# Short constant products of TensorE in the waits at the beginning and end of two mixture-of-experts layers

## Chip, cores, metric

One core of a Trainium2 chip runs the whole program in one launch. The metric is the device time of a run in microseconds (us); lower is better. Five engines work side by side and wait for each other through semaphores: TensorE (PE; its weight loads are PEld), VectorE (DVE), ScalarE (ACT), GpSimd (POOL) and SyncE (SP, which issues most DMAs).

## What is computed

The reference is a chain of ten layers on 256 tokens of width 1024, in float32: gated linear attention, a mixture of experts (MoE), differential attention, a second MoE, and then twice a feed-forward layer, a mixer and a feed-forward layer. A layer norm stands behind each. The change sits in the two MoE layers:

```python
g_idx = jnp.argmax(g_logits, axis=-1)              # one of 4 groups for each token
top_w, top_i = lax.top_k(jax.nn.softmax(e_logits, axis=-1), 2)   # 2 of the group's 4 experts
...
for e in range(16):
    hdn = jax.nn.silu(t @ w_gate[e]) * (t @ w_up[e])
    y = y + combine[:, e:e + 1] * (hdn @ w_down[e])
```

## The kernel before

**Number format.** Large products run in a fast form of float32: each operand is split into a high part (ACT, a cast) and a low part (DVE, a subtraction; POOL for a few) by `split`, line 107. A product is then three matmuls (hi x hi, lo x hi, hi x lo). A matmul of plain float32 operands, such as the router's, is carried out as two PE instructions. A transpose is one PE instruction against the identity matrix `ident`.

**Weights.** They come in units of 128 x 2048 values (1 MB), one DMA each (line 85, on SP's queue), through a ring of five raw buffers and four split ones. In an MoE `GU` (line 696) multiplies the tokens of a group with an expert's gate and up weights, 512 columns a matmul, and `down` (`mm3`, lines 102 to 104) with the down weights.

**Where an MoE begins** (`moe`, `LN`). The layer norm before it (`_rows`, lines 227 to 241) works on one block of 128 tokens after the other (tb is 0, then 1): DVE adds, ACT squares, POOL takes the root, DVE scales. Eight transposes of a block follow (line 250), ACT copies them out (line 734), and `logits` (line 534) makes 20 router values for each token: 8 float32 products with 20 columns, so 16 PE instructions. `route` picks the group on DVE (lines 539 to 548, with small products at line 546 that count the tokens before each one), and `slots` (line 551) makes the matrix `Pm` that picks a group's tokens. `gather` (line 614) multiplies by it, ACT and DVE copy the rows out (line 615), `gathered_T` (line 622) transposes them, `split` parts them, and `GU` of expert 0 begins. POOL splits the two blocks of activations meanwhile (`xl`, line 107), and DVE the second weight unit.

**Where an MoE ends.** After expert 15's `down` (line 104 is its last matmul) ACT and DVE split the sum (`y_parts`). A branch, `tc.If` at line 791, skips the case of groups over 128 tokens; each engine reads the count and takes the branch itself. `scatter` (lines 644 and 645) then multiplies back into token order, and the next layer's first layer norm, transposes (line 250) and matmuls (`mm_A`, line 295) follow.

**Order of the work.** The kernel is traced by a planner, which simulates the program and fixes the order of the instructions on each engine before it runs. `tc.high_priority(n)` lets instructions go ahead of others that are ready; `tc.issue_after(x)` keeps an engine's instructions behind x. On the chip each engine follows its list in that order. PSUM tiles come from `ps(tag)`: four banks "acc", two "ma", two "mb".

Of the kernel before, what the change touches and what calls it, by code (L numbers as in the profile page):

```python
# [19 lines left out]
P = 128  # L20
T = 256
D = 1024
NK = D // P
# [22 lines left out]
def block_kernel(ctx: ExitStack, tc: tile.TileContext, A: dict, out: bass.AP, stop=None, cap=CAP):  # L46
    nc = tc.nc
    V, S, G, PE = nc.vector, nc.scalar, nc.gpsimd, nc.tensor
# [20 lines left out]
    def ps(tag):  # L69

        return psum.tile([P, 512], F32, tag=tag, name=nm(tag), bufs=4 if tag == "acc" else 2)
# [29 lines left out]
    def mm3(o, lh, ll, rh, rl, start, stop):  # L101
        PE.matmul(o, lh, rh, start=start, stop=False)  # L102
        PE.matmul(o, lh, rl, start=False, stop=False)  # L103
        return PE.matmul(o, ll, rh, start=False, stop=stop)  # L104

    def split(hi, lo, src, sub=V):
        return [S.copy(hi, src), sub.tensor_tensor(lo, src, hi, op=ALU.subtract)]  # L107
# [12 lines left out]
    ident = const.tile([P, P], F32, name="ident")  # L120
# [10 lines left out]
    upper = const.tile([P, P], F32, name="upper")  # L131
    V.tensor_scalar(upper, jp, 0.0, None, op0=ALU.is_gt)
    ones = const.tile([P, P], F32, name="ones")
# [65 lines left out]
    class LN:  # L199
# [45 lines left out]
        def transposed(self, tb, r, put):  # L245
            for q in range(2):
                pt = ps("acc")
                for i in range(4):
                    k = q * 4 + i
                    PE.transpose(pt[:, i * P:(i + 1) * P], r[:, k * P:(k + 1) * P], ident)  # L250
                last = put((slice(None), slice(q * 4, q * 4 + 4), slice(tb * P, tb * P + P)),
                    pt.rearrange("p (a b) -> p a b", a=4))
            return last
# [247 lines left out]
    def moe(layer, ln, wr, rb):  # L501
        XX = new_pair()
        xT = base.tile([P, NK, T], F32, tag="x32", name=nm("x32"))
        Xr = [[t[:, tb * 4:(tb + 1) * 4, :].rearrange("p a b -> p (a b)") for tb in range(2)] for t in XX]
        with ExitStack() as st:
# [8 lines left out]
            oh = c.tile([P, 2, 4], F32, name="oh")  # L514
# [16 lines left out]
            def logits(tb):  # L531
                pl = ps("ma")
                for k in range(NK):
                    PE.matmul(pl[:, :20], xT[:, k, tb * P:(tb + 1) * P], wr[:, k, :], start=k == 0, stop=k == NK - 1)
                return pl

            def route(tb, pl):
                lg = c.tile([P, 20], F32, name=nm("lg"))
                V.tensor_tensor(lg, pl[:, :20], rb, op=ALU.add)
                gmax = c.tile([P, 1], F32, name=nm("gmax"))  # L540
                V.reduce_max(gmax, lg[:, 0:4], axis=AX)
                chosen[:] = [first_max(oh[:, tb, :], lg[:, 0:4], gmax)]

                pp = ps("ma")
                for t in range(tb + 1):
                    PE.matmul(pp[:, 0:4], upper if t == tb else ones, oh[:, t, :], start=t == 0, stop=t == tb)
                V.scalar_tensor_tensor(posp[:, tb, :], pp[:, 0:4], 1.0, oh[:, tb, :], op0=ALU.add, op1=ALU.mult)
                routed[tb] = (lg, gmax)

# [57 lines left out]
            def gather(Pg, rows, banks=("acc", "acc")):  # L607

                p = [ps(banks[h]) for h in range(2)]
                for h in range(2):  # L610
                    sl = slice(h * 512, (h + 1) * 512)
                    for tb in range(2):
                        for i in range(2):
                            PE.matmul(p[h], Pg(tb), Xr[i][tb][:, sl], start=tb + i == 0, stop=tb + i == 2)
                    (S.copy if h == 0 else V.tensor_copy)(rows[:, sl], p[h])

            def gathered_T(rows, put, banks=("acc", "acc")):
                for h in range(2):
# [14 lines left out]
            def y_tile():  # L633
                t = base.tile([P, 2, D], F32R, tag="x32", name=nm("yhl"))
                return t[:, 0, :], t[:, 1, :]

            def scatter(PT, yh, yl, banks=("acc", "acc")):

                res = []
                for tb in range(2):  # L640
                    res.append([ps(banks[h]) for h in range(2)])
                    for h in range(2):
                        sl = slice(h * 512, (h + 1) * 512)
                        PE.matmul(res[tb][h], PT[:, tb * P:(tb + 1) * P], yh[:, sl], start=True, stop=False)
                        PE.matmul(res[tb][h], PT[:, tb * P:(tb + 1) * P], yl[:, sl], start=False, stop=True)
                return res

            def add(res):
# [18 lines left out]
            ycur = [None]  # L667

            def down(e, hh, hl, PT):

                if e % 4 == 0:
                    ycur[0] = [ps("acc"), ps("acc")]
                for n in range(2):
                    dh, dl = unit()
                    order = [(fb, half) for fb in range(2) for half in range(2)]
                    if e == 15 and n == 1:
                        order.sort(key=lambda o: o[1])
                    for fb, half in order:
                        f = n * 2 + fb
                        s = slice(fb * 1024 + half * 512, fb * 1024 + half * 512 + 512)  # L680
                        mm3(ycur[0][half], hh[:, f, :], hl[:, f, :], dh[:, s], dl[:, s],
                            e % 4 == 0 and f == 0, e % 4 == 3 and f == 3)
                if e % 4 == 3 and PT is not None:
                    add(scatter(PT, *y_parts(ycur[0], *y_tile())))

# [15 lines left out]
            def prepare(g):  # L701
                Pg = lambda tb: Pm[:, tb, g, :]
                if g:
                    for tb in range(2):
                        slots(tb, g)
                rows = base.tile([P, D], F32, tag="x32", name=nm("xrow"))
                gather(Pg, rows)
                return rows, Pg

            gathered = []  # L710
# [18 lines left out]
            for tb in range(2):  # L729
                with tc.high_priority(200):  # L730
                    r = ln.rows(tb)
                    if tb:
                        parts(0, G, *ln.alone)
                    act = ln.transposed(tb, r, lambda sl, p: S.copy(xT[sl], p))
                    if tb:
                        with tc.issue_after(ln.last.ins):
                            route(0, lgs[0])
                            slots(0, 0)
                        behind[:] = chosen
                        u0.append(unit())  # L740
                    lgs.append(logits(tb))
# [10 lines left out]
            for e in range(16):  # L752
                g = e // 4
                if e % 4 == 0:
                    xg, Pg = nxt
                pg_ = GU(xg, "ma", None if e else u0)
                with tc.issue_after(middle[0].ins):
# [10 lines left out]
                    if e % 4 == 0:  # L768
                        cs = group_weights(Pg, g, "")
                        PT = group_PT(Pg, "")  # L770
# [7 lines left out]
                h = w.tile([P, 512], F32, tag="h", name=nm("h"))  # L778
# [6 lines left out]

            hT = hidden_T(pend[1])
            down(15, *hT, None)
            behind[:] = hidden_last
            y = y_parts(ycur[0], *y_tile())
            n_max = nc.values_load(cnti[0:1, 0:1], min_val=0, max_val=T)  # L790
            with tc.If(n_max > cap):
                for g in range(4):
# [13 lines left out]
                    for e in range(g * 4, g * 4 + 4):  # L806
# [13 lines left out]
                        p = ps("ma")  # L820
# [10 lines left out]
                    t = [w.tile([P, D], F32R, tag=f"xg{i}", name=nm("yf")) for i in range(2)]  # L831
                    add(scatter(PT, *y_parts(yacc, *t), ("ma", "mb")))
            accs = scatter(pend[2], *y)
        return LN(gb, accs)


# [879 lines left out]
```

## Time and profile before

| | us |
|---|---|
| median of 3 runs (lowest, highest) | 1894.28 (1893.7, 1896.81) |
| the profiled execution: its time | 1896.91 |
| the profiled execution: its span | 1895.1 |
| busy in that span: PE, DVE, ACT, POOL | 1850.2, 1302.2, 1102.1, 90.3 |

The span goes from the first to the last instruction of the profiled execution; 1.8 us of the time lie around it. A matmul's record includes the time until its result has landed, so that matmuls that follow each other overlap: the distance between their starts, not their length, is what each costs. TensorE's clock has two levels, 2.4 GHz (granted share 1.00) and 1.2 GHz (0.50). In rows of the order of time a row such as "x8" merges eight instructions, and what stands in brackets is the idle time of the engine before it and what ended that.

### The profile page before, as it was taken

Reading aid. Unit: us, or ns where it says so; the run is one execution under the profiler, and the core shown is the slowest. Engines: PE = TensorE matmul, PEld = TensorE weight load, DVE = VectorE, ACT = ScalarE, POOL = GpSimd, SP = SyncE. Lnnn points to the kernel's source line nnn. Section 1 sums busy time; section 2 is a strip of 40 time slices with the busy share of each in tenths; the row PEclk is TensorE's granted clock in tenths of the full one; section 3 lists DMA queues with packets and bytes.
Section 4 is the critical chain, followed back from the end, with each engine's and each line's share of the span. In section 5 each row is a group of like instructions: output and inputs, shape, how many; then the busy total and the mean of one; then the engine's idle time right before and its main releaser. Section 6 shows DMA issues by size and latency. Waiting matters only on the chain.

```text
span 1895.1 us, 28347 instructions
## 1 busy us (share of the span) xinstructions
PE 1850.2 (98%) x11262; PEld 1624.7 (86%) x11262; DVE 1302.2 (69%) x2029; ACT 1102.1 (58%) x1642; POOL 90.3 (5%) x91
## 2 busy tenths in 40 slices
PE   8989999998999999998999999999999999999998
PEld 6778888886887888887999998999999999989997
DVE  6469899885569898997555587644564457865544
ACT  6356777765666777775444486644454446754442
POOL 0030000001012000001000100100010001010000
PEclk9989999999998999999999999999999999999999
DMA  8538999995426999986554462445545555425440
GB/s 347 179 124 327 348 343 340 347 355 189 155 92 229 362 341 342 344 337 263 223 183 174 174 243 90 182 177 197 201 166 190 200 200 199 175 90 222 181 173 25
DMA packets 63728, 427.78 MB, mean 226 GB/s; under 512 B 8105, under 2 KB 10705, under 8 KB 12642
## 3 DMA queue, kind: packets, MB, share of 16 engines
q1 hardware_dynamic: 56592, 408.45, 57.5%
q10 hardware_dynamic: 6994, 17.43, 2.7%
q8 instruction: 91, 1.49, 0.3%
q14 instruction: 51, 0.42, 0.1%
HBM read 424.79 MB, written 2.63 MB: 226 GB/s over the span
## 4 chain that ended last, share of the span: by engine, by line
PE 52%; ACT 1%; DVE 0%; issue 0%; DVEq 0%; POOLq 0%; POOL 0%
PE acc L104 6%; PE acc L103 6%; PE acc L102 6%; PE mb L103 4%; PE ma L104 4%; PE ma L102 4%; PE mb L104 4%; PE ma L103 4%; PE mb L102 4%; PE ma L295 3%; PE mb L295 3%; PE acc L1081 1%; PE acc L1462 1%; PE mb L1441 1%; ACT hi L107 1%; PE ma L1240 0%
## 5 line engine op out<-in xcount | busy, mean ns | idle before, releaser
L107 DVE TENSOR_TENSOR lo<-raw,hi 128x1024 fp32r<-128x1024 f32 x758 | 891.2, 1220 | 212.4 <-ACT hi L107 206.5
L107 ACT CAST hi<-raw 128x1024 fp32r<-128x1024 f32 x776 | 772.7, 1050 | 259.1 <-PE acc L104 103.0
L102 PE MATMUL acc<-hi,hh 128*128 128x512 f32 x576 | 226.4, 393 | 1.3 <-ACT hh L107 1.3
L103 PE MATMUL acc<-lo,hh 128*128 128x512 f32 x576 | 226.8, 394 | 0.0
L104 PE MATMUL acc<-hi,hl 128*128 128x512 f32 x576 | 220.5, 394 | 0.0
L102 PE MATMUL mb<-xh,hi 128*128 128x256 f32 x608 | 172.3, 283 | 0.0
L104 PE MATMUL ma<-xh,lo 128*128 128x256 f32 x608 | 172.2, 283 | 0.0
L103 PE MATMUL mb<-xl,hi 128*128 128x256 f32 x608 | 172.2, 283 | 0.0
L104 PE MATMUL mb<-xh,lo 128*128 128x256 f32 x608 | 172.1, 283 | 0.0
L103 PE MATMUL ma<-xl,hi 128*128 128x256 f32 x608 | 172.0, 283 | 0.0
L102 PE MATMUL ma<-xh,hi 128*128 128x256 f32 x608 | 172.0, 283 | 0.0
L696 PE MATMUL mb<-hi,xg 128*128 128x512 f32 x512 | 166.9, 393 | 0.0
L696 PE MATMUL ma<-hi,xg 128*128 128x512 f32 x512 | 166.8, 394 | 0.0
L1131 DVE TENSOR_TENSOR h<-mb,sg 128x256 f32<-128x256 f32 x72 | 30.3, 421 | 162.9 <-PE mb L104 162.9
L102 PEld LDWEIGHTS acc<-hi,hh 128*128 128x128 f32 x576 | 108.5, 188 | 23.2 <-ACT hh L107 1.8
L104 PEld LDWEIGHTS acc<-hi,hl 128*128 128x128 f32 x576 | 107.3, 188 | 23.0
L103 PEld LDWEIGHTS acc<-lo,hh 128*128 128x128 f32 x576 | 108.2, 188 | 20.7
L102 PEld LDWEIGHTS ma<-xh,hi 128*128 128x128 f32 x608 | 115.6, 190 | 3.5
L103 PEld LDWEIGHTS ma<-xl,hi 128*128 128x128 f32 x608 | 115.6, 190 | 3.1
L104 PEld LDWEIGHTS ma<-xh,lo 128*128 128x128 f32 x608 | 115.6, 190 | 1.0 <-issue 0.6
L103 PEld LDWEIGHTS mb<-xl,hi 128*128 128x128 f32 x608 | 115.8, 190 | 0.0
L102 PEld LDWEIGHTS mb<-xh,hi 128*128 128x128 f32 x608 | 115.7, 190 | 0.0
(390 smaller groups left out, 3427.6 us busy)
## 6 DMA issues: line engine op xcount, KB each, us to landing
raw<-in_wts SPq DMA_DIRECT2D x387, 1024.0 KB, 5.5
gb<-in_lnp ACTq DMA_DIRECT2D x10, 1024.0 KB, 4.7
bias_dram<-bias_once ACTq DMA_DIRECT2D x1, 1536.0 KB, 9.0
x<-in_xT SPq DMA_DIRECT2D x2, 512.0 KB, 6.0
raw<-in_wts SPq DMA_DIRECT2D x2, 512.0 KB, 8.4
ax<-in_x ACTq DMA_DIRECT2D x1, 1024.0 KB, 12.7
Tb<-bias_dram ACTq DMA_DIRECT2D x1, 1024.0 KB, 13.5
gn<-in_a_g_norm ACTq DMA_DIRECT2D x1, 512.0 KB
```

The source lines that it names most:

```text
L102: PE.matmul(o, lh, rh, start=start, stop=False)
L103: PE.matmul(o, lh, rl, start=False, stop=False)
L104: return PE.matmul(o, ll, rh, start=False, stop=stop)
L107: return [S.copy(hi, src), sub.tensor_tensor(lo, src, hi, op=ALU.subtract)]
L295: last = PE.matmul(o[:, :n], x[part][:, k, ts_], w[:, kk * n:kk * n + n], start=i == 0 and blocks[0][1] == 0, stop=i == len(terms) - 1 and ...
L696: last = PE.matmul(o, xg[part][:, half * 4 + kk, :], weights[:, kk * 512:kk * 512 + 512], start=half == 0 and i == 0, stop=half == 1 and i ...
L1081: PE.matmul(accs[tb][h], hTs[fb][a][:, ts_], dw[b][:, s], start=False, stop=i == len(terms) - 1)
L1131: V.tensor_tensor(h, pu[:, :T], sg, op=ALU.mult)
L1441: PE.transpose(pt[:, i * P:(i + 1) * P], pr[:, i * P:(i + 1) * P], ident)
L1462: PE.matmul(oacc[qb][i * 64:i * 64 + 64, g * 2 + r0 // 2, :], vv[:, kb, bs * P + g * 64:bs * P + g * 64 + 64], pT[:, i * 2 + j, :], start= ...
```

## The change

A helper `idle(n, after, bank)` makes n float32 products of `ident` with the constant `ones` (128 x 128, 128 columns) into a PSUM tile that nobody reads, behind the instruction `after`, with priority 150. In each MoE it is called seven times: 8 products behind the logits of each block, 3 behind the transposes of block 1, 4 behind the counting products of block 1, 2 behind the gather of group 0, 9 behind the last matmul of expert 15, and 18 behind the last matmul of the scatter: 52 products an MoE. The calls inside `logits`, `route` and the loop over tb stand within a priority of 200 already. The other edits only hand on the last instruction of a helper.

```diff
--- before.py
+++ after.py
@@ -103,6 +103,14 @@
         PE.matmul(o, lh, rl, start=False, stop=False)
         return PE.matmul(o, ll, rh, start=False, stop=stop)
 
+    def idle(n, after, bank="mb"):
+
+        t = ps(bank)
+        with tc.issue_after(after.ins), tc.high_priority(150):
+            for _ in range(n):
+                after = PE.matmul(t[:, :P], ident, ones, start=True, stop=True)
+        return after
+
     def split(hi, lo, src, sub=V):
         return [S.copy(hi, src), sub.tensor_tensor(lo, src, hi, op=ALU.subtract)]
 
@@ -247,7 +255,7 @@
                 pt = ps("acc")
                 for i in range(4):
                     k = q * 4 + i
-                    PE.transpose(pt[:, i * P:(i + 1) * P], r[:, k * P:(k + 1) * P], ident)
+                    self.turned = PE.transpose(pt[:, i * P:(i + 1) * P], r[:, k * P:(k + 1) * P], ident)
                 last = put((slice(None), slice(q * 4, q * 4 + 4), slice(tb * P, tb * P + P)),
                     pt.rearrange("p (a b) -> p a b", a=4))
             return last
@@ -531,7 +539,9 @@
             def logits(tb):
                 pl = ps("ma")
                 for k in range(NK):
-                    PE.matmul(pl[:, :20], xT[:, k, tb * P:(tb + 1) * P], wr[:, k, :], start=k == 0, stop=k == NK - 1)
+                    last = PE.matmul(pl[:, :20], xT[:, k, tb * P:(tb + 1) * P], wr[:, k, :],
+                                     start=k == 0, stop=k == NK - 1)
+                idle(8, last)
                 return pl
 
             def route(tb, pl):
@@ -543,7 +553,9 @@
 
                 pp = ps("ma")
                 for t in range(tb + 1):
-                    PE.matmul(pp[:, 0:4], upper if t == tb else ones, oh[:, t, :], start=t == 0, stop=t == tb)
+                    last = PE.matmul(pp[:, 0:4], upper if t == tb else ones, oh[:, t, :], start=t == 0, stop=t == tb)
+                if tb:
+                    idle(4, last)
                 V.scalar_tensor_tensor(posp[:, tb, :], pp[:, 0:4], 1.0, oh[:, tb, :], op0=ALU.add, op1=ALU.mult)
                 routed[tb] = (lg, gmax)
 
@@ -611,8 +623,9 @@
                     sl = slice(h * 512, (h + 1) * 512)
                     for tb in range(2):
                         for i in range(2):
-                            PE.matmul(p[h], Pg(tb), Xr[i][tb][:, sl], start=tb + i == 0, stop=tb + i == 2)
+                            last = PE.matmul(p[h], Pg(tb), Xr[i][tb][:, sl], start=tb + i == 0, stop=tb + i == 2)
                     (S.copy if h == 0 else V.tensor_copy)(rows[:, sl], p[h])
+                return last
 
             def gathered_T(rows, put, banks=("acc", "acc")):
                 for h in range(2):
@@ -634,6 +647,8 @@
                 t = base.tile([P, 2, D], F32R, tag="x32", name=nm("yhl"))
                 return t[:, 0, :], t[:, 1, :]
 
+            added = []
+
             def scatter(PT, yh, yl, banks=("acc", "acc")):
 
                 res = []
@@ -642,7 +657,7 @@
                     for h in range(2):
                         sl = slice(h * 512, (h + 1) * 512)
                         PE.matmul(res[tb][h], PT[:, tb * P:(tb + 1) * P], yh[:, sl], start=True, stop=False)
-                        PE.matmul(res[tb][h], PT[:, tb * P:(tb + 1) * P], yl[:, sl], start=False, stop=True)
+                        added[:] = [PE.matmul(res[tb][h], PT[:, tb * P:(tb + 1) * P], yl[:, sl], start=False, stop=True)]
                 return res
 
             def add(res):
@@ -678,8 +693,8 @@
                     for fb, half in order:
                         f = n * 2 + fb
                         s = slice(fb * 1024 + half * 512, fb * 1024 + half * 512 + 512)
-                        mm3(ycur[0][half], hh[:, f, :], hl[:, f, :], dh[:, s], dl[:, s],
-                            e % 4 == 0 and f == 0, e % 4 == 3 and f == 3)
+                        added[:] = [mm3(ycur[0][half], hh[:, f, :], hl[:, f, :], dh[:, s], dl[:, s],
+                                        e % 4 == 0 and f == 0, e % 4 == 3 and f == 3)]
                 if e % 4 == 3 and PT is not None:
                     add(scatter(PT, *y_parts(ycur[0], *y_tile())))
 
@@ -704,7 +719,9 @@
                     for tb in range(2):
                         slots(tb, g)
                 rows = base.tile([P, D], F32, tag="x32", name=nm("xrow"))
-                gather(Pg, rows)
+                last = gather(Pg, rows)
+                if not g:
+                    idle(2, last)
                 return rows, Pg
 
             gathered = []
@@ -732,6 +749,8 @@
                     if tb:
                         parts(0, G, *ln.alone)
                     act = ln.transposed(tb, r, lambda sl, p: S.copy(xT[sl], p))
+                    if tb:
+                        idle(3, ln.turned)
                     if tb:
                         with tc.issue_after(ln.last.ins):
                             route(0, lgs[0])
@@ -785,6 +804,7 @@
 
             hT = hidden_T(pend[1])
             down(15, *hT, None)
+            idle(9, added[0])
             behind[:] = hidden_last
             y = y_parts(ycur[0], *y_tile())
             n_max = nc.values_load(cnti[0:1, 0:1], min_val=0, max_val=T)
@@ -831,6 +851,7 @@
                     t = [w.tile([P, D], F32R, tag=f"xg{i}", name=nm("yf")) for i in range(2)]
                     add(scatter(PT, *y_parts(yacc, *t), ("ma", "mb")))
             accs = scatter(pend[2], *y)
+            idle(18, added[0])
         return LN(gb, accs)
```

## Rows read from the trace of the kernel before

**Rows 1.** The view of cores: span and mean granted clock.

```profile
core 0: 1895.1 us, clock 0.986
```

**Rows 2.** The view of stretches, for the four in which an MoE begins or ends at the lower clock. Columns: from:to, us, then busy us and instructions of PE, PEld, DVE, ACT and POOL, the granted clock, the DMA engines' share, GB/s.

```profile
127.40:144.50 17.10, 14.38 (x50) 11.26 (x49) 16.19 (x79) 9.56 (x12) 8.62 (x6) 0.50 0.34 125
441.40:448.30 6.90, 6.35 (x19) 4.99 (x20) 6.12 (x13) 3.26 (x5) 4.34 (x3) 0.51 0.28 87
574.50:591.60 17.10, 14.40 (x50) 11.56 (x51) 16.28 (x79) 9.56 (x12) 9.28 (x6) 0.50 0.35 124
888.60:892.00 3.40, 3.40 (x18) 3.12 (x16) 3.40 (x9) 2.61 (x4) 3.39 (x2) 0.50 0.00 0
```

**Rows 3.** The same view, for the stretches just before the clock fell, and one (432.00) after which it did not.

```profile
124.00:127.40 3.40, 1.02 (x9) 0.82 (x8) 2.73 (x6) 2.07 (x3) 1.81 (x2) 1.00 0.00 0
432.00:435.30 3.30, 1.29 (x6) 0.72 (x4) 1.39 (x2) 1.11 (x2) 0.00 (x0) 1.00 0.72 293
437.30:441.40 4.10, 0.17 (x2) 0.03 (x1) 3.23 (x8) 1.24 (x2) 1.42 (x2) 1.00 0.00 2
571.10:574.50 3.40, 1.96 (x16) 1.85 (x16) 2.66 (x7) 2.76 (x4) 0.88 (x2) 1.00 0.00 0
884.80:888.20 3.40, 0.15 (x2) 0.04 (x1) 2.60 (x8) 1.24 (x2) 2.09 (x5) 1.00 0.01 2
```

**Rows 4.** Instructions in order of time, where the first MoE ends. Columns: start, us, engine, line, operation, out<-in, shapes, count, [idle before <- what ended it]. Between the rows at 443.85 and 451.49 there are 24 matmuls of line 295, 12 of them from 448.74 on.

```profile
435.34 0.47 PE L644 MATMUL acc<-yhl,PT 128*128 128x512 f32 x1 [2.05 <-DVEq L791]
...
441.37 1.94 PE L250 MATMUL acc<-ident,ax 128*128 128x128 f32 x8 [3.93 <-DVE ax L241]
...
443.85 0.79 PE L295 MATMUL acc<-hi,xh 128*128 128x512 f32 x1 [0.55 <-DVE xl L107]
...
447.20 1.41 DVE L241 SCALAR_TENSOR_TENSOR ax<-acc,rstd,gb 128x512 f32<-128x512 f32 x2 [0.73 <-POOL rstd L238]
...
448.74 0.39 PE L295 MATMUL acc<-hi,xh 128*128 128x512 f32 x1
...
451.49 1.03 PE L250 MATMUL acc<-ident,ax 128*128 128x128 f32 x8
```

**Rows 5.** The same view, where the second MoE ends. From 889.59 to 896.51 there are 48 matmuls of line 295, 11 of them before 892.07.

```profile
882.82 0.47 PE L644 MATMUL acc<-yhl,PT 128*128 128x512 f32 x1 [1.82 <-DVEq L791]
...
888.17 1.77 PE L250 MATMUL acc<-ident,ax 128*128 128x128 f32 x8 [3.25 <-DVE ax L241]
...
889.59 0.58 PE L295 MATMUL ma<-hi,xh 128*128 128x256 f32 x1
...
892.07 0.28 PE L295 MATMUL ma<-lo,xh 128*128 128x256 f32 x1
...
896.51 1.03 PE L250 MATMUL acc<-ident,ax 128*128 128x128 f32 x8
```

**Rows 6.** The same view, where the first MoE begins. Between 142.07 and 144.66 six matmuls of line 696 start, the first included.

```profile
122.65 1.86 PE L534 MATMUL ma<-route_w,x 128*128 128x20 f32 x16
...
129.68 3.58 PE L534 MATMUL ma<-route_w,x 128*128 128x20 f32 x16
...
130.27 3.39 POOL L107 TENSOR_TENSOR xl<-ax,xh 128x1024 fp32r<-128x1024 f32 x1 [0.46 <-ACT xh L107]
...
131.36 2.33 DVE L565 TENSOR_TENSOR tmp<-lg,oh 128x16 f32<-128x16 f32 x1
...
136.89 0.59 PE L546 MATMUL ma<-oh,upper 128*128 128x4 f32 x2 [0.51 <-DVE m L577]
...
138.41 0.76 PE L614 MATMUL acc<-xh,Pm 128*128 128x512 f32 x1 [0.93 <-DVE Pm L551]
...
140.56 0.69 DVE L615 COPY xrow<-acc 128x512 f32<-128x512 f32 x1
...
142.07 0.79 PE L696 MATMUL ma<-hi,xg 128*128 128x512 f32 x1
...
144.66 0.40 PE L696 MATMUL ma<-hi,xg 128*128 128x512 f32 x1
```

**Rows 7.** The same view, where the second MoE begins. From 589.92 to 591.72 four matmuls of line 696 start, the first included.

```profile
579.39 2.34 DVE L565 TENSOR_TENSOR tmp<-lg,oh 128x16 f32<-128x16 f32 x1
...
586.25 0.77 PE L614 MATMUL acc<-xh,Pm 128*128 128x512 f32 x1 [1.00 <-DVE Pm L551]
...
589.92 0.79 PE L696 MATMUL ma<-hi,xg 128*128 128x512 f32 x1
...
591.72 0.40 PE L696 MATMUL ma<-hi,xg 128*128 128x512 f32 x1
```

**Rows 8.** Float32 products of 128 columns elsewhere in the kernel, at the full clock: the view of one line (line 984, 12 products a call, min/median/max of one record in ns), and eight such instructions in the order of time.

```profile
L984 PE MATMUL ma<-v,wTs x24: 271/275/275, 547.5 to 554.2; 128*128 128x128 f32 x24
...
547.47 1.06 PE L984 MATMUL ma<-v,wTs 128*128 128x128 f32 x8
```

**Rows 9.** The view of waits from 145 to 432 us: SP's queue, PE, and the longest of ACT's. Columns: who waits <- for whom: us in total, times, longest.

```profile
SPq L85 <- DVE lo L107: 253.6, 92, 14.3
...
PE acc L102 <- ACT hh L107: 0.7, 1, 0.7
...
ACT hi L107 <- PE mb L696: 22.5, 27, 2.2
```

## The prediction

> **What bounds the kernel now.** I read the cores first, for the clock: 0.986 over the span [rows 1], so for some 2.8% of it TensorE ran at 1.2 GHz. Stretches show where: four of them, 44.5 us in all, stand where an MoE begins or ends, and PE is busy for 38.5 us of that [rows 2]. The stretches ahead show what PE did before each fall: 3.9 and 3.25 us of nothing where an MoE ends, and 1 to 2 us of small work beside some 2 us of waiting where one begins. After 1.29 us of 512-column matmuls and a wait of 2.05 us the clock stayed up [rows 3, 4]. Between these places, in the experts, PE waits for next to nothing; the others wait for it, ACT's casts for buffers that PE frees and SP's weight DMAs for buffers behind those [rows 9]. So whatever PE gains at the edges, the weight stream can follow, and it stays in the end time.
>
> But 38.5 us at half speed are not 19 us to win. In the order of time one has to look at each place for what is late. Where the first MoE ends, PE is: from 443.85 to the transposes at 451.49 there is no gap [rows 4]. The same holds for the second, 889.59 to 896.51 [rows 5]. Where an MoE begins it is mostly DVE. Its small operation at 131.36 takes 2.33 us for 16 elements a row: it stands still until POOL's split, 130.27 to 133.66, is through, and the whole routing of block 1 queues behind it. It is so in the second MoE as well (579.39) [rows 6, 7]. Only the last step there, the first `GU` matmuls, runs at PE's pace.
>
> **What an idle product costs.** Line 984 makes 12 float32 products a call and shows 24 records: two instructions a product. Eight of them take 1.06 us with a record of 0.275 us, so (1.06 - 0.275) / 7 = 0.112 us from start to start [rows 8]. A product is 0.224 us, and 2, 3, 4, 8, 9 and 18 of them are 0.45, 0.67, 0.90, 1.79, 2.02 and 4.03 us. At the lower clock the router's instructions, whose pace is 0.11 us at the full one, follow each other at (3.58 - 0.37) / 15 = 0.214 [rows 6]; I take that for the idle ones too: 0.43 us a product. The page "TensorE: Matmul & The Clock Gate" of the Trainium skill, section "Back-to-back issue gap", puts a sustained pair of weight load and 128-column matmul at about 81 ns; the row above says 112. By the page the 18 products would take an estimated 2.9 us, and the sum below would be 0.6 us better.
>
> **The sum, edit by edit.**
>
> End of the first MoE. The 9 products start when the last `down` matmul has streamed, 0.16 us before it lands at 433.29, so at 433.13; the last one lands at 433.13 + 17 x 0.112 + 0.275 = 435.31. The scatter waits until 435.34 for the branch [rows 4]. The branch of PE itself now stands behind nine products more, and no row prices that step by itself: at least nothing, at most a wait like the whole present one, 2 us. I take 0.2, since the rows leave the products and the wait equal. The 18 products begin 0.17 us before the scatter's end and take 4.03 of the 4.10 us up to the transposes [rows 4]: free. If the clock then stays up, the start at 443.85 stays, since it waits for DVE's low part; the 24 matmuls to 451.49 took 7.64 us, and the last twelve of them 2.75, 0.229 each, so 24 take 5.50: 2.14 won. The rows of block 1 are scaled by 448.61 [rows 4], so the transposes can come at 449.4. **-1.9.** Next late: ACT's cast behind these transposes, as now.
>
> End of the second. The 9 products land at 880.84 + 1.90 + 0.275 = 883.02, against a scatter at 882.82, and the same 0.2 for the branch: +0.4. The wait for the transposes is only 3.25 + 0.17 = 3.42 us, so the 18 products outlast it by 0.61: +0.6. Eleven matmuls at the lower clock, 2.48 us, become 11 x 0.12 = 1.32: -1.16. The eight transposes give 0.1 [rows 5]. **-0.25.** The planner may put the surplus products behind the transposes, in the 1 us gap there; then it is -0.85.
>
> Beginning of the first. The 8 products behind the logits of block 0 (1.79 us) fit into the 2.4 us in which PE idles before the transposes [rows 3], the 3 behind those into the wait for the routing. The logits of block 1 take 1.86 us and not 3.58, and the 8 products behind them fill what that frees. None of this moves the end while DVE stands behind POOL. The counting product at 136.89 waits for DVE and the gather at 138.41 for `Pm`; the 4 products between take 0.90 of some 1.3 us [rows 6]. From there on it is PE's: the gather's second half, DVE's copy (now at 140.56, which DVE's own queue lets come only 0.1 sooner), the transposes of half the size: 0.4 sooner at `GU`, less 0.2 for the 2 products behind the gather. Six `GU` matmuls, 142.07 to 144.66, 2.59 us, become 6 x 0.229 = 1.37: -1.2. **-1.4.** Bounds: nothing, where the clock falls once more in between; above, the -3.7 of the second rival. I take the value for a clock that stays up: the waits left over are under 2 us with 512-column matmuls on either side, nearest to the row that stayed up [rows 3].
>
> Beginning of the second, in the same way: 4 matmuls, 1.80 us, become 0.92, and 0.3 before them [rows 7]. **-1.2.**
>
> The bank: the tiles come from "mb", which only PE writes here; no other engine is waited for. The instructions add no DMA and no operand. SP, ACT, DVE and POOL get nothing new; their order is the planner's, and no row can price a new order: I take 0, with 2 us to either side, about half of what the sum is.
>
> Sum: -1.9 - 0.25 - 1.4 - 1.2 = -4.75. The profiled execution took 1896.91 us, so 1892.2; it lay 2.6 over the median of the runs. Against the median: 1894.28 - 4.75 = **1889.5**.
>
> **The rivals.**
>
> 1. The ends win, the beginnings don't: the clock falls again between the short waits, or DVE sets the start even of `GU`. For it: the logits, 16 instructions of 20 columns, were at work just ahead of one fall [rows 3], and they stay. Against: 8 wide products now stand behind each. -2.15: 1892.1, which a measurement cannot tell from no change (that is about 0.2%, 3.8 us, here).
>
> 2. More is won: with PE quick, the planner's order or the place of POOL's split no longer hold the routing, and the logits of block 1 (1.7 us) and its transposes (0.6) count too in both: -4.6 more, 1884.9. Against: DVE's stall behind POOL does not hang on PE.
>
> 3. Slower: in the beginnings the clock falls before the logits of block 1 and stays down, and PE, which takes its list in order, must do the idle products at 0.43 us. Then these logits end at 133.1 as now, the 8 products at 136.5, the counting and the first half of the gather (0.5 us and four matmuls at 0.43, as `GU`'s are there [rows 6]) at 138.7, the counting of block 1 at 139.2 and not 137.4, the 4 products at 140.9: the gather's second half comes 2.5 us late in each MoE. With the ends as above, +5.0 - 2.15 = +2.9: 1897.1; with the branch at its upper bound in both ends, 1900.7. It decides from where the clock falls ahead of 131 us.
>
> 4. The planner drops or scatters them into places where nothing waits, and the clock is as before: 1894.3.
>
> **How the numbers follow.** The forecast gets 0.45 (own range 1887.2 to 1892.0, by 2 us for the planner's order; 0.32 of it below 1890.5). Rival 1 gets 0.15, rival 2 0.16, rival 3 0.20 (0.11 of it above 1898.1), rival 4 0.04. Faster by over 0.2%: 0.32 + 0.16 = 0.48. Slower: 0.11. The rest, 0.41, is within it. For 8 in 10 the range goes from rival 2's value to rival 3's: 1884.8 to 1897.3; outside stay about 0.06 below and 0.10 above.
>
> **What would show it.** Right: the granted clock of the span at 0.995 or more; a clock of 1.00 where the MoEs end, the 24 matmuls there in 5.5 us, and some 2 us less from the scatter to the second transposes; scatters 0.2 to 0.4 us later behind `down`; DVE's operation of line 565 still 2.3 us long; the six `GU` matmuls 0.23 apart; idle products 0.112 apart. Wrong: a clock of 0.50 between 124 and 145 us, idle products 0.214 apart, and a gather later than now (rival 3); DVE's routing free of POOL (rival 2); transposes of line 250 that wait behind idle products by more than 0.6 us; or a gap in the experts, where PE waits for a low part of a weight, which would take back what the edges gave.

## The result, and the profile after

The changed kernel takes 1910.22 us (median of 4 runs, 1908.94 to 1910.84), the kernel before 1894.40 in the same comparison: a ratio of 1.0078 [1.0066, 1.0090], 15 us slower. The forecast was 1889.5, the range ended at 1897.3. Its rival on the slower side does not describe it either: the clock is up where that rival has it down. One execution of an experiment below (the order without idle products) took 3685 us, at a clock of 1.00, and its difference leaves it out.

The view of cores after:

```profile
core 0: 1907.2 us, clock 0.994
```

The clock rose from 0.986 to 0.994 [rows 1] and the time rose with it. The view of stretches shows where the clock was, with the columns of [rows 2]: both beginnings, the new low stretches behind them, and the scatter of the first MoE.

```profile
124.00:139.00 15.00, 12.98 (x95) 11.01 (x93) 13.73 (x54) 10.27 (x14) 9.63 (x7) 1.00 0.39 142
170.40:177.20 6.80, 4.71 (x14) 3.97 (x15) 3.10 (x8) 1.18 (x2) 0.00 (x0) 0.50 0.84 335
443.50:446.90 3.40, 3.40 (x15) 3.11 (x14) 2.60 (x9) 1.24 (x2) 0.69 (x2) 0.50 0.00 0
571.00:586.00 15.00, 14.06 (x102) 12.11 (x101) 13.46 (x24) 8.55 (x13) 8.11 (x6) 1.00 0.37 142
624.40:631.20 6.80, 5.16 (x15) 4.22 (x15) 2.81 (x5) 1.18 (x2) 0.00 (x0) 0.50 0.80 317
```

The 17.1 us at 1.2 GHz are gone from both beginnings. In their place stand two stretches of 6.8 us inside the experts, 30 us behind each beginning, where the kernel before had none.

To see where time is lost, I put the same instruction of both traces side by side (start in us) and read the difference as it grows and shrinks:

| instruction | before | after | shift | step, and the forecast of it |
|---|---|---|---|---|
| POOL's root ahead of the first MoE | 125.40 | 124.61 | -0.8 | |
| expert 0, first up matmul | 145.12 | 140.97 | -4.2 | -3.4 (-1.4) |
| expert 5, first gate matmul | 221.06 | 225.43 | +4.4 | **+8.5** (0) |
| last `down` matmul | 432.90 | 437.27 | +4.4 | 0 |
| transposes of block 1 | 451.49 | 457.38 | +5.9 | **+1.5** (-1.9) |
| POOL's root ahead of the second MoE | 568.37 | 573.35 | +5.0 | -0.9 |
| expert 0, first up matmul | 592.64 | 594.78 | +2.1 | -2.8 (-1.2) |
| last `down` matmul | 880.62 | 890.70 | +10.1 | **+7.9** (0) |
| transposes of block 1 | 896.51 | 908.55 | +12.0 | **+2.0** (-0.25) |

From there the shift stays at 12.0. (The medians differ by 15.8, because the profiled execution of before lay 2.5 above its median and that of after 1.3 below its own.) The beginnings won more than forecast. Behind each of them 8 us were lost, and each end lost where it should have won.

**The loss inside the experts.** The view of waits from 139 to 200 us, then from 590 to 660, PE's lines:

```profile
PE acc L606 <- DVE comb L600: 3.8, 1, 3.8
PE acc L673 <- DVE h L798: 1.1, 1, 1.1
PE ma L711 <- DVE lo L115: 0.8, 1, 0.8
...
PE acc L606 <- DVE comb L600: 2.5, 1, 2.5
PE acc L673 <- DVE h L798: 1.7, 1, 1.7
```

PE waits for `comb`, the experts' weights that `weigh` makes on DVE. Before, they were there in time. Instructions in the order of time, before (columns as in [rows 4]):

```profile
140.24 0.22 DVE L587 TENSOR_SCALAR pr<-pr,gs 128x4 f32<-128x4 f32 x1
140.56 0.69 DVE L615 COPY xrow<-acc 128x512 f32<-128x512 f32 x1
141.17 0.15 DVE L526 TENSOR_REDUCE fm<-oh 128x1 f32<-128x4 f32 x1
...
143.81 4.62 DVE L107 TENSOR_TENSOR lo<-raw,hi 128x1024 fp32r<-128x1024 f32 x4
148.36 0.22 DVE L527 TENSOR_SCALAR oh<-oh,fm 128x4 f32<-128x4 f32 x1
...
155.16 0.17 DVE L588 TENSOR_TENSOR comb<-oh,pr 128x16 f32<-128x16 f32 x1
...
160.09 0.28 PE L594 MATMUL acc<-comb,Pm 128*128 128x4 f32 x2
```

And after, the same place:

```profile
161.52 0.16 DVE L598 TENSOR_TENSOR pr<-pr,oh 128x4 f32<-128x4 f32 x1
161.60 0.15 DVE L592 TENSOR_REDUCE m<-pr 128x1 f32<-128x4 f32 x1
161.66 1.21 DVE L115 TENSOR_TENSOR lo<-raw,hi 128x1024 fp32r<-128x1024 f32 x1
162.80 0.22 DVE L599 TENSOR_SCALAR pr<-pr,gs 128x4 f32<-128x4 f32 x1
162.93 0.22 DVE L532 TENSOR_SCALAR oh<-pr,m 128x4 f32<-128x4 f32 x1
163.06 0.15 DVE L595 TENSOR_TENSOR m<-m,m 128x1 f32<-128x1 f32 x1
163.13 2.35 DVE L115 TENSOR_TENSOR lo<-raw,hi 128x1024 fp32r<-128x1024 f32 x2
165.40 0.17 DVE L600 TENSOR_TENSOR comb<-oh,pr 128x16 f32<-128x16 f32 x1
...
171.13 0.17 DVE L600 TENSOR_TENSOR comb<-oh,pr 128x16 f32<-128x16 f32 x1
171.36 0.59 PE L606 MATMUL acc<-comb,Pm 128*128 128x4 f32 x2 [3.75 <-DVE comb L600]
...
173.08 1.09 PE L673 MATMUL acc<-ident,h 128*128 128x128 f32 x4 [1.13 <-DVE h L798]
```

`weigh` is a chain of short operations, each waiting for the one before it. In the kernel before DVE does nearly all of it in its waits ahead of the experts: when the low parts of the weights begin (143.81), five operations are left. They come out between low parts of 1.2 us, and the last, `comb` of block 1, comes at 155.16. In the shorter beginning DVE's list has fewer of them ahead of the experts: 29 operations of the two blocks' chains are still to come when the low parts begin at 140.52, 24 low parts run among them, and `comb` of block 1 comes at 171.13. PE waits 3.75 us for `comb`, 1.13 for `h` behind it and 0.8 for a low part, its clock falls at the end of the first of these waits (170.4), and as PE is busy for 4.71 of the 6.8 us at half speed, these cost up to 2.4 more: 8.0, of the 8.5 in the table. In the second MoE the same sum is 2.5 + 1.7 + 0.8 + 2.6 = 7.6 of 7.9.

**The loss at the ends.** The same view where the first MoE ends, after:

```profile
437.27 0.39 PE L104 MATMUL acc<-hi,hl 128*128 128x512 f32 x1
437.50 2.17 PE L111 MATMUL mb<-ones,ident 128*128 128x128 f32 x18
442.24 0.47 PE L659 MATMUL acc<-yhl,PT 128*128 128x512 f32 x1 [2.56 <-PEq L811]
...
444.77 5.19 PE L111 MATMUL mb<-ones,ident 128*128 128x128 f32 x36
449.79 1.04 PE L258 MATMUL acc<-ident,ax 128*128 128x128 f32 x8
```

The scatter starts 4.6 us behind the last `down` matmul and not 2.05 [rows 4], and what it waits for is no longer DVE but PE's own sequencer (PEq), in the branch. How long that branch takes stands in the view of its line, in ns, before and then after:

```profile
L791 PEldq COMPARE_BRANCH  x2: 3772/3800/3828, 429.6 to 877.1; - x2
```

```profile
L811 PEldq COMPARE_BRANCH  x2: 3687/3744/3802, 438.1 to 891.5; - x2
```

It takes 3.7 to 3.8 us in both. Before, the sequencer reaches it 3.74 us ahead of the landing of the last `down` matmul, since queued matmuls keep the array busy meanwhile (3.74 us are 16 of them, at 0.232 each), and it is over when they are. After, the places in the queue are taken by 18 short instructions of 0.112 us instead of matmuls of 0.232, and the branch begins at 438.12, 0.46 us behind that landing. The page "Runtime: NRT & Kernel Launch" of the Trainium skill, section "Instruction fetch mechanics", says that a taken branch to a target outside what has been fetched must wait for the code. The trace agrees: in the branch one packet of 16 KB comes on a DMA queue of kind "instruction", from 430.56 to 432.03 before and from 439.50 to 440.40 after, and the branch is over 1.35 and 1.52 us behind it.

### The profile page after: what moved, and what is told of

Same layout as the page of the kernel before. It is cut to its first block, busy times and chain, and to the rows that moved or that the text cites. A ratio compares the mean times of both kernels' runs of the same rounds, so it can differ in the third digit from the quotient of the medians.

```text
span 1907.2 us, 28771 instructions
## 1 busy us (share of the span) xinstructions
PE 1862.5 (98%) x11470; PEld 1638.5 (86%) x11470; DVE 1301.7 (68%) x2029; ACT 1102.5 (58%) x1642; POOL 88.9 (5%) x91
## 4 chain that ended last, share of the span: by engine, by line
PE 51%; ACT 1%; DVE 0%; ACTq 0%; issue 0%; DVEq 0%; POOLq 0%
PE acc L104 6%; PE acc L103 6%; PE acc L102 6%; PE mb L103 4%; PE ma L104 4%; PE ma L102 4%; PE mb L104 4%; PE ma L103 4%; PE mb L102 4%; PE ma L303 3%; PE mb L303 3%; PE acc L1102 1%; PE acc L1483 1%; PE mb L1462 1%; ACT hi L115 1%; PE ma L1261 0%
```

## The experiments

Theory A: the experts' loss is the chain that comes late on DVE. Theory D: the ends' loss is the branch that lost its cover, the matmuls queued ahead of it. Rivals: the loss comes from the idle products themselves, by their places in PE's list or by the clock. Differences below are ratios of the runs times the time of before, with 95% intervals.

**Beginnings alone, ends alone.** In one kernel the two calls at the ends are taken out, in the other the four at the beginnings.

```diff
-            idle(9, added[0])
...
-            idle(18, added[0])
```

> Only the idle products of the beginnings (8 behind each block's logits, 3 behind the transposes, 4 behind the counting, 2 behind the gather); none at the ends. Theory A: with shorter waits ahead of the first GU matmul, VectorE does fewer of the small operations that work out the experts' weights in those waits; the rest go one by one between low parts of weights of 1.2 us each, so comb comes at 171 instead of 155 us, TensorE waits 3 to 4 us for it, and its clock falls behind that wait. By the shifts between the traces (from 0.8 us early to 4.9 late in the first MoE, from 5.0 to 10.4 late in the second) this kernel is some 11 us slower than before: about 1905. Rival B: the loss is made at the ends (the products ahead of the branch and those ahead of the transposes); then this one is 4 to 5 us faster than before, 1890. Rival C: idle products cost the clock wherever they stand; then it is slower, and the clock is down before TensorE waits for comb and not behind it.

Measured: 1906.91 us, +9.7 [6.4, 12.9]. PE's waits for `comb` are those of the whole change, 3.8 and 2.5 us, and the clock falls behind them (172.8 and 626.7). As theory A had it, in size too.

> Only the idle products of the ends (9 behind the last down matmul, 18 behind the scatter). Theory A: the shifts between the traces grow by 2.5 us at the first end and by 1.7 at the second, less 2.4 that the layer in between gave back: between 1 and 5 us slower than before, 1895 to 1899, comb at 155 us and no wait for it as in the kernel before. Rival B, all the loss at the ends: 1909. My prediction: 2 us faster, 1892.

Measured: 1899.28 us, +3.2 [1.3, 5.1]; `comb` at 155.2, no wait for it. The forecast of this half was 2 us faster. The two halves make 12.9 of the 15.

**The chain ahead of the low parts.** The later low parts are queued behind the chain's last operation, once with the idle products of the beginnings, once without any.

```diff
-                V.tensor_tensor(comb[:, tb], o[:, :, None].to_broadcast([P, 4, 4]),
+                return V.tensor_tensor(comb[:, tb], o[:, :, None].to_broadcast([P, 4, 4]),
...
-                            weigh(tb)
+                            wts = weigh(tb)
...
+                        behind.append(wts)
```

> The idle products of the beginnings, and the low parts of the weights from the third unit on are queued on VectorE behind the last operation of the chain (comb of block 1), so that the small operations stand together ahead of them. Theory A: comb at about 148 us, no wait of TensorE for it in either MoE, no fall of its clock at 170 and 624 us, and the start of GU stays early: 3 to 9 us faster than before, about 1888, against some 1905 without the order. Rival B (the idle products' own places in TensorE's order delay the experts): no better than without the order, 1905. Rival C (clock): between, as the clock still falls for some 7 us in each MoE, 3 us each.

Measured: 1892.84 us, -2.7 [-4.5, -0.9], 14 us less than without the order. `comb`, by the view of its tile:

```profile
L600 DVE TENSOR_TENSOR comb<-oh,pr x2: 168/172/176, 143.9 to 146.2; 128x16 f32<-128x16 f32 x2
```

PE no longer waits for it, and the clock stays up from 139 to 439 us with every idle product of the beginnings in place. The same products at the same calls cost nothing here, which excludes both rivals for this half.

> The kernel before with that order of VectorE alone, no idle product. Theory A: no difference that can be told, within 2 us of before, since TensorE did not wait for comb there. Rival: the order by itself gains (then the kernel with idle products owes its time to it) or costs some us, since the first low parts come 2 to 3 us later.

Measured: 1897.81 us, +1.3 [-0.6, 3.2]. The order gains nothing that can be told by itself.

**The loss without an idle product.** The kernel before, with the chain kept out of the waits.

```diff
-                            weigh(tb)
+                            with tc.issue_after(gathered[1].ins):
+                                weigh(tb)
```

> The kernel before, with no idle product, but the small operations for the experts' weights (the chain that ends in comb) are all queued on VectorE behind the last low part of the gathered rows, so that none of them runs in the waits ahead of the first GU matmul. Theory A: the chain then goes between the low parts of weights as in the changed kernel, with more of it left over: comb of block 1 at 170 us or later and not 155, TensorE waits for it in both MoEs and its clock falls there, at least as slow as the idle products of the beginnings alone (11 us): 1905 to 1920. If the loss needs the idle products (their places in TensorE's order, or the activity), this kernel costs nothing: 1894 to 1896.

Measured: 1924.57 us, +29 [26, 33], beyond what I expected. `comb` of block 1 comes at 180.6, and PE's waits in the first MoE are:

```profile
PE acc L594 <- DVE comb L588: 5.6, 2, 5.3
PE ma L696 <- DVE lo L107: 4.7, 2, 4.0
PE acc L658 <- DVE h L780: 1.1, 1, 1.1
```

So a late chain makes such a loss without any idle product (PE's 4.7 us for low parts, which this edit holds back too, are a part of the 29). With the run of the chain ahead of the low parts, the idle products of the beginnings cost time only by making the chain late.

**The two ends apart.** One kernel has only the 9 products, one only the 18.

> Only the 9 idle products behind the last down matmul, ahead of the branch. Theory D: TensorE's branch takes 3.8 us in the trace, before and after. In the kernel before TensorE's sequencer reaches it 4.3 us before the last down matmul lands (TENSOR_LOAD at 428.95), with 16 queued 512-column matmuls to run meanwhile, and the branch is over at 433.38, ahead of the scatter. The 18 instructions of the idle products take those places in the queue and run 0.112 us each and not 0.23, so the branch starts when the last down matmul does (437.52 in the changed kernel) and the scatter stands behind it: 2.6 us later at each end, about 5 us slower than before, 1899 to 1901. My prediction: 0.2 to 0.4 us an end, 1895. A rival (the clock, down at the scatter, makes the loss): the branch would stand where it did, and the scatter would start 2.05 us behind the last down matmul.

Measured: 1900.95 us, +5.5 [3.6, 7.4]. The scatters start 4.74 and 4.38 us behind the landing of the last `down`, 2.7 and 2.6 later than before.

> Only the 18 idle products behind the scatter. Theory D: the branch is covered as before, the scatter starts 2.05 us behind the last down matmul, the products fit ahead of the transposes at the first end, the 24 matmuls behind them take 5.5 us and not 7.6, and at the second end the products outlast the wait by 0.6 us: 2 us faster than before, with the products' cost, 1892 to 1894. Rival E (the 18 products themselves are the loss, since the transposes stand behind them by 2 us at each end): 1896 to 1899.

Measured: 1892.12 us, -3.2 [-5.1, -1.3]. Where the first MoE ends:

```profile
434.31 0.47 PE L656 MATMUL acc<-yhl,PT 128*128 128x512 f32 x1 [2.05 <-DVEq L803]
...
436.26 4.18 PE L111 MATMUL mb<-ones,ident 128*128 128x128 f32 x36
440.37 1.31 PE L258 MATMUL acc<-ident,ax 128*128 128x128 f32 x8
```

The products end when the transposes can start. Up to the transposes of block 1 this end gains 2.04 us (forecast 2.1 for these products alone, without the 0.2 for the branch). At the second end the first transposes are 0.61 late against the scatter (forecast 0.6), and those of block 1 come 0.6 sooner (forecast 0.66, without the 0.4 for the nine products). So the 18 products were costed rightly, and the loss of the ends is the 9. In the changed kernel the 18 came late behind the late scatter, with the clock down at 443.5.

**The branch.** Six, four and two products, and two runs that move another engine's branch. One execution each, but for the four.

> Four idle products and not nine behind the last down matmul, none elsewhere. Theory D (places in the queue): 8 short instructions take the places of 8 long ones, so the branch is over 8 x 0.232 = 1.9 us later against the last down matmul, 0.2 + 1.9 = 2.1 us behind its end, and the scatter waits as long as that for its low part in any case: 2.05 us. No loss, within 1 us of before. If the branch's cost came with any idle product ahead of it (a switch of the engine, not places), the scatter is 2.6 us late here too, and the kernel 5 us slower.

> Six idle products behind the last down matmul and nothing else. By places in the queue, 12 short instructions for long ones, TensorE's branch starts 12 x 0.232 = 2.8 us later against the last down matmul, and SyncE's, which does not move, stands 1.2 us ahead of it. If the branch takes 3.8 us again, it is over 3.0 us behind the last down matmul and the scatter 1 us late at each end. If the 6.2 us with four products came from SyncE's branch just ahead (0.1 to 0.3 us there), the branch takes between 3.8 and 6.2 us here. If it came from a small number of short instructions in the queue, 6.2 again.

> Two idle products behind the last down matmul and nothing else. By places: the branch starts 4 x 0.232 = 0.9 us later against the last down matmul, 0.6 us ahead of SyncE's, takes 3.8 us and is over 1.1 us behind the last down matmul; the scatter comes 2.05 us behind, as before. If any idle product ahead makes the branch 6.2 us long, it is over 3.5 us behind, and the scatter is 1.5 us late.

The four-product kernel took 1901.40 us, +7.6 [4.9, 10.2], the kernels with six and two 1897.95 and 1895.21. All times below are against the landing of the last `down`, at the first and the second end; "packet" is the start of the 16 KB packet in the branch:

| products | branch begins | packet | takes | is over | scatter |
|---|---|---|---|---|---|
| 0 | -3.74, -3.92 | -2.73, -2.51 | 3.83, 3.77 | +0.1, -0.2 | 2.05, 1.82 |
| 2 | -2.81, -2.99 | -1.79, -2.07 | 3.55, 3.37 | +0.7, +0.4 | 2.05, 1.81 |
| 4 | -1.88, -2.06 | +2.02, +1.79 | 6.24, 6.23 | +4.4, +4.2 | 4.68, 4.56 |
| 6 | -0.94, -1.13 | +1.43, +1.63 | 4.86, 5.16 | +3.9, +4.0 | 4.23, 4.35 |
| 9 | +0.46, +0.28 | +1.80, +1.58 | 3.90, 3.78 | +4.4, +4.1 | 4.74, 4.38 |

Up to six products the beginning follows theory D to 0.1 us: 0.93 us later for every four instructions, 0.232 each. Two products are free, as expected. With four the branch should have been over at 1.9, and it was not: from four on it is over some 4.2 us behind the last `down`, whenever it began. My expectation for four was wrong by that.

SyncE's branch stands 0.1 to 0.3 us ahead of PE's in that run, so I held it back; then I moved ScalarE's, which stood 3.3 to 3.8 us ahead of the branch's end in the runs with four to nine products.

```diff
+            held = dram.tile([1, 4], F32, name=nm("held"))
+            nc.sync.dma_start(held, y[0][0:1, 0:4].bitcast(F32))
             n_max = nc.values_load(cnti[0:1, 0:1], min_val=0, max_val=T)
```

> Four idle products behind the last down matmul, as in the kernel whose branch took 6.2 us, and SyncE sends four numbers of y (its first high part, cast behind the last down matmuls of one half) to memory ahead of its branch, so that its branch comes some 2 us behind TensorE's and not 0.2 ahead. If the order of the two branches sets the length, TensorE's takes 3.4 to 3.9 us again, is over 1.9 us behind the last down matmul, and the scatter starts 2.05 us behind it, as before, and not 4.6. If the number of short instructions sets it, 6.2 us and a scatter 4.6 us behind, as without the hold.

> The kernel before with the same hold of SyncE's branch and no idle product: what the hold costs by itself. TensorE's branch already comes 1.6 us ahead of SyncE's, so it and the scatter stay where they are; SyncE's next weight transfers come 1 to 2 us later, behind buffers that wait for longer than that: 1893 to 1897.

> Four idle products behind the last down matmul, and the high part of y's second half cast by VectorE in place of ScalarE, so that ScalarE's last cast follows the first half's accumulation and its branch comes 1.4 us earlier, 0.8 us ahead of the landing of the last down matmul (0.6 behind it in all runs so far). In the runs with four or more products TensorE's branch is over 3.3 to 3.9 us behind ScalarE's, as long as a branch alone, whenever it began. If ScalarE's branch restarts it, it is over some 2.9 us behind the last down matmul here and takes about 4.8 us; if ScalarE's branch has no part in it, it is over 4.1 to 4.4 us behind again and takes 6.2.

With SyncE's branch 1.5 us behind PE's, PE's takes 6.20 and 6.39 us (1901.36 us; the control without products 1895.91). With ScalarE's 1.4 us sooner, it takes 6.21 and 6.15 (1901.56 us). So neither engine's branch sets the length.

What the length goes with is the 16 KB packet. The view of DMA queues (queue and kind: packets, MB, share) has one such packet in the branch of before (429.55 to 433.38), and with four products none in the first 3.88 us of the branch (429.41 to 433.29) and one in the next (433.29 to 434.30):

```profile
q8 instruction: 1, 0.02, 2.4%
q8 instruction: 1, 0.02, 5.9%
```

Queue q8 brings TensorE's instructions: 91 packets in the kernel before for 11262 matmuls and as many loads, one for some 250 of them. In all 34 such branches of TensorE, two in each of the 17 kernels here, there is one packet, and the branch is over 1.34 to 1.56 us behind its landing. The packet starts 0.9 to 1.4 us behind the branch's beginning, but with four or six products 2.4 to 4.0: there it starts 0.5 to 0.8 us ahead of the landing of a 1 MB weight transfer, which SP issues 2.55 us ahead of the landing of the last `down` in every one of these kernels. That the packet is held by this transfer is not shown, since no run moves the transfer; the run that holds SP's branch leaves it where it was.

**Both gains together.** The kernel has the beginnings with the order, and the 18 products at the ends.

> The idle products of the beginnings, the low parts queued behind comb, and the 18 products behind the scatter; none ahead of the branch. Theories A and D: the gain of the beginnings with the order (2.8 us in the medians) and that of the 18 products alone (2.8 us) stand in different places and add up: some 5.6 us faster than before, about 1889, with no fall of the clock at the ends. If the two come from the same clock (its falls only move from one place to the other), the sum is no better than either: 1892.

Measured: 1891.76 us, -3.4 [-5.1, -1.7]: faster than both kernels, but less than the 5.9 of the two gains (2.7 and 3.2). With intervals of 1.7 to 1.9 us on each of the three, that shortfall is not clear of noise; the trace shows where a part of it can lie. The clock is not the reason: it is down once, for 6.8 us, at 567. The lead over the kernel before grows from 5.3 us at the beginning of the second MoE to 7.4 at its first up matmul, and is 5.0 at its last `down`. The view of waits from 583 to 877 us has these lines, while in the kernel before (590 to 882 us) ACT waits for no DMA, and for `lo` only a weight load of PE, 0.2 us:

```profile
ACT hi L115 <- DMA raw<-in_wts: 2.7, 3, 1.3
...
PE ma L711 <- DVE lo L115: 1.0, 2, 0.8
```

In the last kernel the low parts are queued behind the chain only from the fifth unit on.

> The idle products of the beginnings and the 18 behind the scatter, with the low parts queued behind comb only from the fifth unit on, so that the four low parts that TensorE needs first are not held back by the chain. Theory A: comb still comes ahead of the group's weights (at about 152 us), and the 1 to 2 us that the experts take back in each MoE with the full order (waits of 0.8 and 0.5 us for low parts) shrink: 1 to 3 us faster than with the full order, 1889 to 1891. If the low parts behind comb are what is late there, no difference: 1892.

Measured: 1895.50 us, -0.2 [-1.9, 1.5], against my expectation. The clock falls at 165 us, behind a wait of 1.9 us for ACT's `hh` (the high part of what `down` multiplies), and the lead of 3.6 us at the first gate matmul is 1.0 from the fourth expert on.

## Why the prediction was wrong

**The step that failed** is "SP, ACT, DVE and POOL get nothing new; their order is the planner's, and no row can price a new order: I take 0, with 2 us to either side". It cost 8.5 and 7.9 us. A row could have given a price. The waits that the change was to shorten were not empty: DVE's rows in them are the chain of `weigh`. The five operations left over before took from 148.36 to 155.16, about 1.7 us each, as they share DVE with the low parts, and `comb` stood only 4.9 us ahead of its reader at 160.09: by that rate, an estimate, three operations more in that place and PE waits. I named a gap in the experts as what "would take back what the edges gave", but gave it no chance, and looked for it in the low parts and not in `comb`. (The forecast's own range, 1887.2 to 1892.0, is a little wider than 2 us to either side, 1887.5 to 1891.5; nothing hangs on that.)

**The branch**: "I take 0.2", with 2 us as the upper bound. It was 2.7 and 2.6 (9 products alone), beyond that bound. I asked what the products add to PE's work, 2.02 us in a wait of 2.05, and not what the branch stands behind. It stands behind the queued matmuls that hid its 3.8 us: its record, beginning 3.7 us ahead of their end, was in the trace of before.

**The 18 products** were right in mechanism and size (-2.04 and -0.6 measured, -2.1 and -0.66 forecast for them alone), in a kernel where the scatter isn't late.

**The beginnings** were right in direction and too small: -3.4 and -2.8 up to the first up matmuls, against -1.4 and -1.2. The `GU` matmuls in this gave 1.1 and 0.8, as forecast (1.2 and 0.9); too small were the 0.2 and 0.3 for all that lies ahead of them, which gave 2.2 and 2.1. In the first MoE DVE still stands still behind POOL's split (one low part at 129.46 takes 3.38 us now, in place of the small operation) and goes on 8.2 us behind POOL's root, before and after. Then it turns to block 1's logits 0.2 us later and not 1.3, and the counting products come 0.85 sooner; the stretch from there to `GU`, at the full clock, gives 1.3. So the second rival's 3.7 is near, and one of its reasons, the planner's order in the routing, is a part of it; POOL's split still holds DVE. With the order of the experiments, 1.7 to 2.4 us are taken back in the experts.

**"The weight stream can follow"** was not quite so: with the edges quicker, ACT waits for weight transfers (2.7 us in the second MoE) and PE for low parts, as the run with both gains shows.

**The clock** came out as forecast in the beginnings, 1.00 throughout, and the third rival did not occur. The instructions of idle products follow each other at (4.18 - 0.28) / 35 = 0.111 us (36 in a row, behind the scatter of the 18 products alone), the 0.112 of the sum. The Trainium skill's page "TensorE: Matmul & The Clock Gate", section "Back-to-back issue gap", has 81 ns for a pair of weight load and 128-column matmul; here the measurement decides.

## What to carry to other kernels

When a wait is to be shortened, look first at what the other engines do in it: work that was free there has to go somewhere, and in an order that is fixed beforehand it goes between longer instructions, one at a time. Price it by how many operations are left over and how far ahead of its reader the last one stands. The clock granted is no measure of the time: here it rose by 0.008 while the kernel lost 15 us.

## What was not expected of the hardware

A branch that TensorE takes is 3.3 to 3.9 us long here, and up to 6.4 with four or six short products ahead of it, while its record on the other engines is 0.04 to 0.07 us. Its length goes with a 16 KB packet of TensorE's instructions: in 34 branches of 17 kernels it is over 1.34 to 1.56 us behind that packet's landing. With 16 matmuls of 512 columns queued ahead of it, 3.7 us of work, the branch is hidden. With eight of them and eight short ones it is not: the packet then starts 3.7 to 4.0 us behind the branch's beginning in place of 0.9 to 1.4, near the end of a 1 MB weight transfer, and the branch is over 4.1 to 4.4 us behind the last long matmul.
